# Two-layer stream encoder on one core: keys split once, one reciprocal per head, 9 dummy products, a planner that keeps engines apart at a bank

## The chip, the cores and the metric

The kernel runs on one core of a Trainium2 chip. The metric is the time of one execution on the device in microseconds (us); lower is better. Engines are named as in the profile: PE (matrix products; PEld its weight loads), DVE, ACT and POOL (elementwise work), SP (issues transfers).

## The reference

The program takes 512 tokens of 1024 values through two attention layers, all in float32. Only what bears on the change is quoted.

```python
def diff_dsa_layer(x, ...):               # layer 0
    proj = rms_norm(x, norm_g) @ w_in
    qa, ka, va, qb, kb, vb, qi, ki, wi, gate = split_cols(proj, L0_SIZES)
    o_a = diff_attention(...)             # 4 heads: softmax - lam * softmax
    o_b = dsa_attention(...)              # 8 heads; an indexer picks 128 keys for each query
    return x + (concat(o_a, o_b) * silu(gate)) @ w_o

def dsa_attention(q, k, v, q_idx, k_idx, w_idx, bias_tab, top_k):
    logits = einsum('bqhd,bkd->bqhk', qi_blk, k_idx)         # ki: one key of 64 for 8 heads
    score = einsum('bqh,bqhk->bqk', w_blk, relu(logits))
    _, sel = lax.top_k(score, top_k)
    s = einsum('bqhd,bqkd->bhqk', q_blk, k_sel) * scale      # kb: one key of 64 for 8 heads
    p = softmax(s + bias)

def mla_attention(q_nope, q_rope, k_nope, k_rope, v):        # layer 1, 16 heads
    s = (einsum(q_nope, k_nope) + einsum(q_rope, k_rope)) * scale
    p = softmax(where(chunk_mask, s, -inf))                  # four tiles of 128 queries
    return einsum('bhqk,bkhd->bqhd', p, v)
```

## The kernel before

All values are float32. A product with full precision is made of three fast ones: an operand is split into a high part (`hi_of`, a copy that rounds, on ACT or DVE) and a low part (`lo_of`, a subtraction of the high part, mostly on DVE), and `mm3` adds high*high, high*low and low*high into one bank. A bank is one of 8 accumulators of 128 rows by 512 words in PSUM; PE writes it and ACT and DVE read it. Where a head has only 64 values, `stacks` lays the high part of a query on one half of the 128 rows and its low part on the other half, by four transfers between places in SBUF (`ra<-ra`), so that two products do the work of three (`stacked_scores`). The keys of these products then have to stand in both halves of the rows.

The kernel is first recorded: every call goes into a list (`Schedule.record`) with what it depends on and a price in ns (`cost`). `Schedule.order` then plays the list with these prices on five queues (PE, ACT, DVE, POOL, and the transfers of SP), starts on each free engine the ready operation that was recorded first (with some shifts by `BIAS`), gives out banks and buffers, and picks the engine where there is a choice (`either`, used by `hi_any`, `lo_any`, `vg`). The instructions are written in the order of these starts. On the chip every engine works through its own list in that order; waits on semaphores keep the dependences, and where two engines read one bank, one of them waits for the other. So a change of a price or of one operation can move instructions all through the program.

The stages in the order of time: values and the sum of squares of layer 0 (PE begins with `WARM` dummy products on zeros while the first data arrive); normalised input `H`; the projection of the two keys (`t_proj`, 24 products into one bank), then of the indexer's queries, of four difference heads, of eight sparse heads. The keys `kb` (rows 0 to 63 of the bank) and `ki` (rows 64 to 127) are split in a loop that makes four pairs of `hi_of` and `lo_of` of 64 rows each. The top-k selection runs on DVE (16 rounds of `max` and `match_replace` for three tiles). Gates and the product with `w_o` end layer 0. Layer 1 makes the latent projections, then 16 heads (`head`): for four tiles of queries the scores, `softmax_rows` (DVE adds the mask and takes the minimum; ACT takes the exponential and its sum), a reciprocal on DVE, `scale_rows` on ACT, then ten transposes on PE, and the products with the values. For every fourth head `rope_q` makes four DVE multiplications on 32 rows each, and for every head one DVE addition on 64 rows joins the two halves of the result (`os_`). The sparse heads of layer 0 end with additions on 64 rows by 128 (32 of them).

Of the kernel before, what the change touches and what calls it, by code (L numbers as in the profile page):

```python
# [23 lines left out]
NT = 4  # L24
# [11 lines left out]

TABLE = 2400.0

WARM = 12

SOON = 14000

# [37 lines left out]
class Buf:  # L80


    def __init__(self, arena, words, kind):
        self.arena, self.words, self.kind = arena, words, kind
        self.users, self.used, self.until, self.at, self.turn = 0, 0, 0.0, None, None


class View:
# [47 lines left out]
def _size(ap):  # L136
    n = 1
    for d in ap.shape[1:]:
        n *= d
    return n  # L140
# [47 lines left out]
class Schedule:  # L188
# [65 lines left out]
    def cost(self, key, name, k, wr, rd):  # L254


        n = max(_size(v) for v in wr + rd) if key != "PE" else _size(wr[0])
        psum = any(v.space == PSUM for v in wr + rd)
        if key == "PE":
            if name == "transpose":  # L260
                return 109.0, False
            rows = {F32R: 1, BF16: 1}.get(rd[0].dtype, 4)
            return max(n * rows / 2.4 + {F32R: 13, BF16: 3}.get(rd[0].dtype, 6), 109.0), False
        if name == "dma_start":
            kb = _size(wr[0]) * wr[0].shape[0] * 4 / 1024
            return ISSUE, (kb, RATES[rd[0].space == DRAM, wr[0].space == DRAM, kb >= 256])
        if key == "ACT":
            extra = 93 * (len(rd) - 1) + (93 if "accum_out" in k else 0)
            return _size(wr[0]) * 0.8333 + (52 if rd[0].space == PSUM else 93) + extra, False
        if key == "DVE":  # L270
            if name == "reciprocal":
                return 8.3 * n + 63, False
            fast = name in ("tensor_copy", "tensor_scalar") and not psum
            port = not psum and name not in ("max", "match_replace", "tensor_reduce", "memset")
            if name == "tensor_scalar" and n == 1:
                return 180.0 if len(rd) > 2 else 70.0, port
            return n * (0.521 if fast else 1.0417) + 68 + 60 * sum(_size(v) == 1 for v in rd if n > 1), port
        if key == "POOL":
            if k.get("op") == ALU.pow:
                return 380.0 + 160 * n, True  # L280
            if name == "tensor_copy" or name == "tensor_scalar" and n > 4:
                return 0.84 * n + 190, True
            if name == "tensor_scalar":
                return 340.0 if len(rd) > 2 else 200.0, True
            per = {"memset": 0.85, "tensor_tensor": 2.1}.get(name, 2.0)
            return per * n + (40 if name == "memset" else 198), True

    def order(self):
# [71 lines left out]
                arrive(j, lambda e: 0.0)  # L360
        now, done, tick = 0.0, 0, itertools.count()
        while done < n:
            progress = False
            if back and back[0][0] <= now:
                while back and back[0][0] <= now:
                    b = heapq.heappop(back)[2]
# [5 lines left out]
            for e in engines:  # L372
# [4 lines left out]
                while pool[e] and free[e] <= now:  # L377
# [6 lines left out]
                        continue  # L384
                    op = ops[j]
                    if e in port and op[9][c][5] and not port_free(now, e, entry):
                        later.append(entry)
                        continue
                    new = [b for b in op[8] if b.at is None]
# [21 lines left out]
                    src = "DMA" if op[1] == "dma_start" else e  # L411
                    for b in op[8]:
                        b.used += 1
                        b.until = max(b.until, end + LAT[src]["PE"])
                        if b.used == b.users:
                            heapq.heappush(back, (b.until, next(tick), b))
# [12 lines left out]
            if not progress:  # L429
                nxt = [free[e] for e in engines if pool[e] and free[e] > now]  # L430
                nxt += [wait[e][0][0] for e in engines if wait[e] and wait[e][0][0] > now]
                nxt += [back[0][0]] if back else []
                nxt += [t for t in port.values() if t > now]
                assert nxt, "no place left"
                now = min(nxt)
        self.pick, self.end = pick, max(finish)
# [14 lines left out]
def encoder_kernel(ctx, tc, x, xt0, xt, rel_bias, w_t0, w_va, lam_v, subln, w_o0,  # L451
# [15 lines left out]
    def R(words, kind="r"):  # L467
        return sched.alloc(ra, words, kind)
# [304 lines left out]
    def t_proj(stream, cols):  # L773
        w = both(stream.next(), lambda v: v.rearrange("p (k m) -> p k m", k=8))
        b = bank("d")
        for k in range(8):
            mm3(by_tile(b), both(w, lambda v: v[:, k]), cols.k(k), k == 0, k == 7)
        return b
# [2 lines left out]
    G.memset(cmn, 0.0)  # L781
    G.memset(cmn[0:64, 448:512], -BIG)

    b = t_proj(wt0, H)
    kst = []
    for r0 in (0, 64):
        hh, ll = R(512), R(512)
        src = b[r0:r0 + 64]
        for rows in (slice(0, 64), slice(64, 128)):
            hi_of(hh[rows], src)  # L790
            lo_of(ll[rows], src, hh[rows])
        kst.append((hh, ll))
    kb, ki = kst

    def full(b, scale, kind="r", via=False):

# [9 lines left out]
        lo_scaled(ll, b, hh, scale) if scale != 1.0 else lo_of(ll, b, hh)  # L806
        return hl

    def halves(hl):
        return hl[:, 0:512], hl[:, 512:1024]  # L810

    def stacks(b, scale, via=False):

# [103 lines left out]


    mark_dsa = len(sched.ops)
    osum = [F(512) for _ in range(4)]  # L920
    for i in range(NT):
        n = 128 * (i + 1)
# [236 lines left out]
    def head(h, q, vs):  # L1159
        kk = halves(kbuf[h % NK])  # L1160
        hv = h % 8
        prs = []
        for i in range(NT):
            n = 128 * (i + 1)
            sb = bank("s")
            if i:
                mm3(sb[:, 0:n], both(q, lambda v: v[:, tok(i)]), both(kk, lambda v: v[:, 0:n]), True, True)
            else:

                qf, kf = F(128, "qf"), F(128, "qf")  # L1170
                for f, (hh, ll) in ((qf, q), (kf, kk)):
                    vg(lambda e: e.tensor_tensor(out=f, in0=hh[:, 0:128], in1=ll[:, 0:128], op=ALU.add))
                T.matmul(sb[:, 0:128], qf, kf, start=True, stop=True)
            sd, rc = sm(1), sm(1)
            p = softmax_rows(sb, n, mz[:, 512 - n:512], sd)
            V.reciprocal(rc, sd)
            scale_rows(p, rc)
            prs.append(p)

        def turn(blocks, pair):  # L1180
            bt = bank("t")
            for c, (kt, i) in enumerate(blocks):
                T.transpose(bt[:, tok(c)], prs[i][:, tok(kt)], ident)
            bt = bt[:, 0:128 * len(blocks)]
            hi_any(pair[0], bt)
            lo_of(pair[1], bt, pair[0])

        ob = bank("o")
        zz = pbz[h % 2]
        pa, pc = (R(512, "pa"), R(512, "pa")), (R(256, "pc"), R(256, "pc"))  # L1190
        turn([(0, i) for i in range(4)], pa)
        turn([(3, 3), (1, 1), (1, 2), (1, 3)], both(zz, lambda v: v[:, 128:640]))
        turn([(2, 2), (2, 3)], pc)
        parts = [(0, 0, pa), (1, 128, both(zz, lambda v: v[:, 256:640])), (2, 256, pc),
                 (3, 256, both(zz, lambda v: v[:, 0:256]))]
        for kt, o, pair in parts:
            mm(ob[:, o:512], vs[kt][:, hv], pair[0], kt == 0, False)
            mm(ob[:, o:512], vs[kt][:, hv], pair[1], False, kt == 3)
        return ob
# [173 lines left out]
```

## Time and profile before

| | us |
|---|---|
| median of 3 runs (lowest, highest) | 533.37 (532.03, 534.36) |
| the profiled execution | 533.3 |
| its span, first to last instruction | 531.5 |
| PE busy, DVE busy, ACT busy, POOL busy | 520.9, 436.1, 322.7, 128.8 |

The profiled execution's own time is 1.8 us longer than its span and agrees with the median. Busy time of PE is the union of modelled intervals, in which products overlap; busy times of the other engines are sums of instructions.

### The profile page before, as it was taken

Reading aid. Unit: us, or ns where it says so; the run is one execution under the profiler, and the core shown is the slowest. Engines: PE = TensorE matmul, PEld = TensorE weight load, DVE = VectorE, ACT = ScalarE, POOL = GpSimd, SP = SyncE. Lnnn points to the kernel's source line nnn. Section 1 sums busy time; section 2 is a strip of 40 time slices with the busy share of each in tenths; the row PEclk is TensorE's granted clock in tenths of the full one; section 3 lists DMA queues with packets and bytes.
Section 4 is the critical chain, followed back from the end, with each engine's and each line's share of the span. In section 5 each row is a group of like instructions: output and inputs, shape, how many; then the busy total and the mean of one; then the engine's idle time right before and its main releaser. Section 6 shows DMA issues by size and latency. Waiting matters only on the chain.

```text
span 531.5 us, 8612 instructions
## 1 busy us (share of the span) xinstructions
PE 520.9 (98%) x2770; PEld 440.4 (83%) x2770; DVE 436.1 (82%) x1099; ACT 322.7 (61%) x745; POOL 128.8 (24%) x193
## 2 busy tenths in 40 slices
PE   9999899999999999999999999999999999999995
PEld 6998788888788888787889998888888887888885
DVE  5878779999999999669489457799899888998744
ACT  6655662785787976673244235289868858995011
POOL 1010001431447544210012114322231201410311
PEclk9999999999999999999999999999999999999999
DMA  8463657539446014019366103953753535846012
GB/s 287 168 206 102 175 136 201 129 109 255 111 121 182 7 40 159 1 41 349 129 240 208 41 21 99 213 138 92 179 157 106 146 106 132 230 159 218 2 44 115
DMA packets 30144, 73.80 MB, mean 139 GB/s; under 512 B 4072, under 2 KB 9364, under 8 KB 30100
## 3 DMA queue, kind: packets, MB, share of 16 engines
q1 hardware_dynamic: 29812, 72.73, 46.7%
q8 instruction: 22, 0.36, 0.3%
q10 hardware_dynamic: 288, 0.53, 0.3%
q14 instruction: 22, 0.18, 0.1%
HBM read 45.96 MB, written 4.80 MB: 96 GB/s over the span
## 4 chain that ended last, share of the span: by engine, by line
PE 75%; DVE 15%; ACT 5%; issue 3%; DMA 1%; POOL 0%; POOLq 0%; DVEq 0%; ACTq 0%
PE bank L443 75%; DVE fa L443 8%; DVE ra L443 5%; ACT fa L443 4%; DVE ring L443 2%; ACT ra L443 1%; DMA ra<-ra 1%; POOL fa L443 0%; POOLq L1369 0%; POOL ring L443 0%; DVE warm L443 0%; DVEq L1369 0%; ACT ring L443 0%; DVEq L443 0%; ACTq L443 0%
## 5 line engine op out<-in xcount | busy, mean ns | idle before, releaser
L443 PE MATMUL bank<-ra 128*128 128x512 f32 (+4 forms) x2276 | 493.3, 369 | 2.1 <-DMA ra<-ra 1.7
L443 PEld LDWEIGHTS bank<-ra 128*128 128x128 f32 x2276 | 385.5, 189 | 62.4 <-issue 2.5
L443 ACT ACTIVATE fa<-fa,ring 128x128 f32<-128x128 f32 (+3 forms) x244 | 127.5, 557 | 65.4 <-POOL ring L443 32.5
L443 ACT ACTIVATE ra<-fa 128x1024 fp32r<-128x1024 f32 (+7 forms) x121 | 90.3, 771 | 47.0 <-PE bank L443 21.0
L443 DVE TENSOR_TENSOR ra<-fa,ra 128x512 fp32r<-128x512 f32 (+4 forms) x153 | 103.7, 708 | 12.1 <-ACT ra L443 10.7
L443 ACT ACTIVATE fa<-bank 128x512 f32<-128x512 f32 (+4 forms) x106 | 52.0, 500 | 43.6 <-PE bank L443 41.5
L443 DVE TENSOR_TENSOR ra<-bank,ra 128x512 fp32r<-128x512 f32 (+2 forms) x100 | 59.1, 624 | 11.4 <-ACT ra L443 10.5
L443 ACT ACTIVATE ra<-bank 128x512 fp32r<-128x512 f32 (+3 forms) x84 | 45.6, 561 | 36.4 <-PE bank L443 32.0
L443 DVE TENSOR_TENSOR fa<-bank,fa 64x128 f32<-64x128 f32 (+6 forms) x97 | 46.3, 484 | 23.6 <-PE bank L443 20.1
L443 PE MATMUL bank<-ident,fa 128*128 128x128 f32 x352 | 64.0, 274 | 1.1 <-ACT fa L443 0.7
L443 POOL TENSOR_TENSOR fa<-fa 128x256 f32<-128x256 f32 (+3 forms) x49 | 46.7, 960 | 61.3 <-DVE fa L443 42.5
L443 POOL TENSOR_TENSOR ra<-fa,ra 128x512 fp32r<-128x512 f32 (+1 forms) x26 | 33.5, 1296 | 108.9 <-ACT ra L443 101.0
L443 DVE CUSTOM_DVE_ANT_0 fa<-bank,fa 128x128 f32<-128x128 f32 (+3 forms) x128 | 57.8, 479 | 0.8 <-issue 0.2
L443 PEld LDWEIGHTS bank<-ident,fa 128*128 128x128 f32 x352 | 44.5, 140 | 14.3 <-ACT fa L443 4.9
L443 POOL TENSOR_TENSOR ring<-ring,mhalf 128x1 f32<-128x1 f32 (+1 forms) x20 | 14.5, 724 | 74.6 <-DVE ring L443 73.6
L443 POOL TENSOR_TENSOR fa<-ra 128x128 f32<-128x128 f32 x28 | 14.9, 535 | 65.1 <-DMA ra<-ra 36.9
L443 DVE MATCH_REPLACE8 fa<-ring,fa 128x256 f32<-128x256 f32 (+2 forms) x48 | 25.7, 538 | 0.0
L443 DVE MAX8 ring<-fa 128x8 f32<-128x256 f32 (+2 forms) x48 | 25.2, 547 | 0.2
L443 DVE CAST ra<-bank 128x512 fp32r<-128x512 f32 (+1 forms) x36 | 21.4, 618 | 4.1 <-PE bank L443 3.8
L443 ACT ACTIVATION_READ_ACCUMULATOR fa<-fa,ring 128x1 f32 x128 | 24.3, 190 | 0.0
L443 PEld LDWEIGHTS bank<-fa 128*128 128x128 f32 (+1 forms) x114 | 16.7, 188 | 4.1 <-ACT fa L443 0.9
L443 PE MATMUL bank<-fa 128*128 128x128 f32 (+1 forms) x114 | 19.0, 283 | 0.3 <-ACT fa L443 0.2
(55 smaller groups left out, 195.8 us busy)
## 6 DMA issues: line engine op xcount, KB each, us to landing
ra<-ra SPq DMA_DIRECT2D x64, 256.0 KB, 4.9
fa<-in_w_t_dram SPq DMA_DIRECT2D x25, 512.0 KB, 4.5
fa<-in_w_o_dram SPq DMA_DIRECT2D x16, 512.0 KB, 5.5
ra<-ra SPq DMA_DIRECT2D x48, 128.0 KB, 2.5
fa<-in_w_g_dram SPq DMA_DIRECT2D x8, 512.0 KB, 3.7
fa<-in_w_lat_dram SPq DMA_DIRECT2D x4, 672.0 KB, 5.5
fa<-in_w_uq_dram SPq DMA_DIRECT2D x12, 192.0 KB, 3.4
fa<-in_x_dram SPq DMA_DIRECT2D x4, 512.0 KB, 9.1
```

Source lines behind the costliest of these rows:

```text
L443: fn(*[_real(v) for v in a], **{n: _real(v) for n, v in k.items()})
```

## The change

Five edits. `WARM` goes from 12 to 9. The key bank is split once over all 128 rows (`full`), and `ki` and `kb` reach the other half of the rows by transfers of 64 rows by 1024 words: two for `ki`, and later one that puts `kb` over the place of `ki`. In `head` the four sums of a head stand side by side, one reciprocal of 128x4 is taken after the fourth softmax, and the four scalings follow it. In the planner, an operation of ACT or DVE on a bank is held until the other engine's last one on that bank has ended, and a DVE operation that writes fewer than 128 rows costs 95 ns more.

```diff
-WARM = 12
+WARM = 9
...
+        self.last = {}
...
-            return n * (0.521 if fast else 1.0417) + 68 + 60 * sum(_size(v) == 1 for v in rd if n > 1), port
+            return n * (0.521 if fast else 1.0417) + 68 + 95 * (wr[0].shape[0] < 128) + 60 * sum(_size(v) == 1 for v in rd if n > 1), port
...
-            progress = False
+            progress, held = False, []
...
+                    turns = [t + LAT[o][e] for b in op[8] if e != "PE" for o, t in b.last.items() if o != e]
+                    if turns and max(turns) > now:
+                        held.append(max(turns))
                         later.append(entry)
                         continue
...
+                        if isinstance(b.arena, Banks) and e != "PE":
+                            b.last[e] = end
...
-                nxt += [t for t in port.values() if t > now]
+                nxt += [t for t in port.values() if t > now] + held
...
-    b = t_proj(wt0, H)
-    kst = []
-    for r0 in (0, 64):
-        hh, ll = R(512), R(512)
-        src = b[r0:r0 + 64]
-        for rows in (slice(0, 64), slice(64, 128)):
-            hi_of(hh[rows], src)
-            lo_of(ll[rows], src, hh[rows])
-        kst.append((hh, ll))
-    kb, ki = kst
...
+    kall = full(t_proj(wt0, H), 1.0)
+    kix = R(1024)
+    for o in (0, 64):
+        dma(kix[o:o + 64], kall[64:128])
+    ki = halves(kix)
...
     mark_dsa = len(sched.ops)
+    dma(kall[64:128], kall[0:64])
+    kb = halves(kall)
...
-            sd, rc = sm(1), sm(1)
-            p = softmax_rows(sb, n, mz[:, 512 - n:512], sd)
-            V.reciprocal(rc, sd)
-            scale_rows(p, rc)
-            prs.append(p)
+            if i == 0:
+                sd, rc = sm(4), sm(4)
+            prs.append(softmax_rows(sb, n, mz[:, 512 - n:512], sd[:, i:i + 1]))
+        V.reciprocal(rc, sd)
+        for i in range(NT):
+            scale_rows(prs[i], rc[:, i:i + 1])
```

Over the program the counts change by little else: PE has 2702 products for 2705 (the three dummies), SP has three more transfers of 64x1024, DVE has 16 reciprocals of 128x1 for 80 and 28 of 128x4 for 12. The order changes on every engine from the keys on.

On DVE the low parts of the keys were four operations of 64x512 and are one of 128x512; the low part of the first indexer queries, which stands behind them, has three DVE operations between it and `lamneg` where it had five.

On SP at the split of the keys (`ra<-ra 64x512` are the stacks of the indexer's queries, four for each bank; `64x1024` the keys; `in_w_t` weights), before:

```order
L443 DMA fa<-in_w_t_dram 128x1024 x3
L443 DMA ra<-ra 64x512 x2
L443 DMA fa<-in_w_t_dram 128x1024
L443 DMA ra<-ra 64x512 x6
L443 DMA fa<-in_w_t_dram 128x1024 x2
L443 DMA ra<-ra 64x512 x4
```

and of the change:

```order
L453 DMA fa<-in_w_t_dram 128x1024 x3
L453 DMA ra<-ra 64x1024 x2
L453 DMA fa<-in_w_t_dram 128x1024
L453 DMA ra<-ra 64x512 x4
L453 DMA ra<-ra 64x1024
L453 DMA ra<-ra 64x512 x4
L453 DMA fa<-in_w_t_dram 128x1024
```

Two key transfers now go ahead of the first stacks, and the move of `kb` stands between the first and the second four.

On PE from the projections of the first queries (`bank_75`, `bank_73`, `bank_70`) to the first scores of the indexer (`128x256`, `128x384` and `128x512` x2 are the scores of one head), before:

```order
L443 MATMUL bank_75<-ra 128x512 x8
L443 MATMUL bank_73<-ra 128x512 x24
L443 MATMUL bank_70<-ra 128x512 x11
L443 MATMUL bank_76<-ra 128x256 x2
L443 MATMUL bank_77<-ra 128x384 x2
L443 MATMUL bank_74<-ra 128x512 x2
```

and of the change:

```order
L453 MATMUL bank_75<-ra 128x512 x8
L453 MATMUL bank_73<-ra 128x512 x24
L453 MATMUL bank_70<-ra 128x512 x17
L453 MATMUL bank_76<-ra 128x256 x2
L453 MATMUL bank_77<-ra 128x384 x2
L453 MATMUL bank_74<-ra 128x512 x2
```

Six more products of the third projection stand ahead of the first scores.

On DVE in the first heads of layer 1 (`ISA fa,ring` is the mask and minimum of one tile of a softmax, its width the last number; `32x512` are multiplications of `rope_q`), before:

```order
L443 ISA fa,ring<-bank_73,fa 128x512
L443 ISA ring 128x1
L443 RECIPROCAL ring<-ring 128x1
L443 ISA fa,ring<-bank_70,fa 128x256
L443 ISA ring 128x1
L443 ISA fa,ring<-bank_74,fa 128x128
L443 ISA ring 128x1
L443 RECIPROCAL ring<-ring 128x1
L443 TENSOR_TENSOR fa<-bank_72,fa 32x512 x2
L443 RECIPROCAL ring<-ring 128x1
L443 ISA fa,ring<-bank_73,fa 128x384
```

and of the change:

```order
L453 TENSOR_TENSOR fa<-bank_77,fa 32x512
L453 ISA fa,ring<-bank_71,fa 128x128
L453 ISA ring 128x1
L453 ISA fa,ring<-bank_76,fa 128x512
L453 ISA ring 128x1
L453 ISA fa,ring<-bank_72,fa 128x256
L453 ISA ring 128x1
L453 ISA fa,ring<-bank_74,fa 128x128
L453 ISA ring 128x1
L453 TENSOR_TENSOR ra<-bank_73,ra 128x512
L453 RECIPROCAL ring<-ring 128x4
```

The reciprocals that stood one by one behind their tiles became one, which stands behind the first two tiles of the next head. On PE the first transpose of a head stands 53 products behind the head's first score on average over the 16 heads, where it stood 37 behind.

## Rows read from the trace of the kernel before

**Rows 1.** The page, busy time: us, share of the span, instructions.

```profile
PE 520.9 (98%) x2770; PEld 440.4 (83%) x2770; DVE 436.1 (82%) x1099; ACT 322.7 (61%) x745; POOL 128.8 (24%) x193
```

**Rows 2.** Busy time by stretch: us, PE, PEld, DVE, ACT, POOL, granted clock, DMA.

```profile
62.00:220.00 158.00, 157.21 (x824) 131.10 (x822) 148.05 (x430) 109.81 (x291) 58.07 (x94) 1.00 0.45 124
340.00:490.00 150.00, 149.08 (x807) 124.38 (x806) 136.88 (x376) 116.98 (x283) 35.31 (x43) 1.00 0.56 153
500.00:510.00 10.00, 10.00 (x46) 8.28 (x45) 2.50 (x7) 0.00 (x0) 1.17 (x1) 1.00 0.00 0
```

**Rows 3.** Waits of PE and PEld, 50 to 62 us: total us, times, longest.

```profile
PEld bank L443 <- issue: 2.1, 1, 2.1
PE bank L443 <- DMA ra<-ra: 1.7, 1, 1.7
```

**Rows 4.** Waits of PEld, 62 to 220 us.

```profile
PEld bank L443 <- ACT fa L443: 2.6, 5, 0.7
PEld bank L443 <- DVE fa L443: 1.2, 3, 0.4
```

**Rows 5.** Waits of PEld, 340 to 490 us.

```profile
PEld bank L443 <- ACT fa L443: 3.2, 12, 0.6
PEld bank L443 <- DVE ra L443: 1.9, 6, 0.5
PEld bank L443 <- issue: 1.2, 3, 0.5
```

**Rows 6.** The dummies (tile warm): ns min/median/max, first and last start.

```profile
L443 PE MATMUL bank<-warm x12: 606/634/635, 1.2 to 5.8; 128*128 128x512 bf16 x12
```

**Rows 7.** Busy time by stretch at the start (columns as in rows 2).

```profile
5.90:6.90 1.00, 1.00 (x5) 0.91 (x4) 0.92 (x2) 0.47 (x1) 0.00 (x0) 1.00 1.05 364
7.00:8.00 1.00, 1.00 (x10) 1.00 (x10) 0.17 (x1) 0.20 (x1) 0.00 (x0) 1.00 0.92 261
```

**Rows 8.** Timeline of ACT and DVE, 3.5 to 9.4 us: start, length, instruction, idle before.

```profile
3.88 1.03 ACT L443 ACTIVATE ra<-fa 128x256 fp32r<-128x256 f32 x2 [1.43 <-DMA fa<-in_w_va_dram]
7.80 0.72 ACT L443 ACTIVATE ra<-fa 128x512 fp32r<-128x512 f32 x1 [1.43 <-DMA fa<-in_xt_dram]
...
4.94 0.75 DVE L443 SCALAR_TENSOR_TENSOR ra<-fa,ra 128x512 fp32r<-128x512 f32 x1 [0.19 <-ACT ra L443]
```

**Rows 9.** Timeline of ACT, DVE, SP and PE, 44 to 57 us.

```profile
44.37 1.18 ACT L443 ACTIVATE ra<-bank 64x512 fp32r<-64x512 f32 x2
46.30 0.59 ACT L443 ACTIVATE ra<-bank 64x512 fp32r<-64x512 f32 x1 [0.75 <-DVE ra L443]
...
50.42 0.69 DVE L443 TENSOR_TENSOR ra<-bank,ra 128x512 fp32r<-128x512 f32 x1
51.03 1.28 DVE L443 TENSOR_TENSOR ra<-fa,ra 128x512 fp32r<-128x512 f32 x2
...
51.14 3.72 SPq L443 DMA_DIRECT2D ra<-ra  x6
...
55.79 4.43 PE L443 MATMUL bank<-ra 128*128 128x256 f32 x23 [1.73 <-DMA ra<-ra]
```

**Rows 10.** The chain that ended last, 30 to 57 us: start, length, what.

```profile
51.14 4.51 DMA ra<-ra
```

**Rows 11.** Groups of instructions by form: busy us, mean ns, idle before.

```profile
L443 DVE TENSOR_TENSOR fa<-bank,fa 64x128 f32<-64x128 f32 x32 | 9.0, 282 | 0.8 <-ACT fa L443 0.4
L443 DVE RECIPROCAL ring<-ring 128x1 f32<-128x1 f32 x80 | 10.7, 152 | 1.9 <-ACT fa L443 1.1
L443 ACT ACTIVATE fa<-fa,ring 128x384 f32<-128x384 f32 x60 | 35.7, 606 | 6.1 <-DVE ring L443 6.0
```

**Rows 12.** Timeline of DVE, 433 to 445 us.

```profile
435.24 3.48 DVE L443 TENSOR_TENSOR fa<-bank,fa 128x512 f32<-128x512 f32 x5
...
443.97 0.16 DVE L443 RECIPROCAL ring<-ring 128x1 f32<-128x1 f32 x1
444.05 0.68 DVE L443 CUSTOM_DVE_ANT_0 fa<-bank,fa 128x512 f32<-128x512 f32 x1
```

More of the change, by code (lines that the diff above doesn't have):

```diff
@@ L386, in order @@
                     if e in port and op[9][c][5] and not port_free(now, e, entry):
+                        later.append(entry)
+                        continue
+                    turns = [t + LAT[o][e] for b in op[8] if e != "PE" for o, t in b.last.items() if o != e]
+                    if turns and max(turns) > now:
+                        held.append(max(turns))
                         later.append(entry)
@@ L782, in encoder_kernel, with halves @@
     G.memset(cmn[0:64, 448:512], -BIG)
-    b = t_proj(wt0, H)
-    kst = []
-    for r0 in (0, 64):
-        hh, ll = R(512), R(512)
-        src = b[r0:r0 + 64]
-        for rows in (slice(0, 64), slice(64, 128)):
-            hi_of(hh[rows], src)
-            lo_of(ll[rows], src, hh[rows])
-        kst.append((hh, ll))
-    kb, ki = kst
+    def halves(hl):
+        return hl[:, 0:512], hl[:, 512:1024]
     def full(b, scale, kind="r", via=False):
@@ L807, in full @@
         return hl
-    def halves(hl):
-        return hl[:, 0:512], hl[:, 512:1024]
+    kall = full(t_proj(wt0, H), 1.0)
[3 more added lines that the diff above has]
+    ki = halves(kix)
     def stacks(b, scale, via=False):
```

## The prediction

> **What bounds the kernel now.** I read the busy times of the page first: PE is busy in 98% of the span, the next engine, DVE, in 82% [rows 1]. A busy PE is not yet a PE at its peak, so I then looked for a stretch in which nothing is waited for. From 500 to 510 us PE runs products of 512 columns alone, 46 in 10 us, one per 0.217 us [rows 2], which is 512 columns at the 2.4 GHz level of its clock, granted 1.00. So the question is how far the other stretches fall short, and the waits of PE and of its weight loads tell it: one wait of 1.7 us at the first indexer scores [rows 3], some small ones in the attention of layer 0 [rows 4], 3.8 us in the two rows shown, and some in layer 1 [rows 5], 6.3 us in three rows. That is about 12 us of 531.5. Everything else is PE's own work, of which the change removes three dummies and nothing more.
>
> There is a rule that would read this otherwise. The Trainium skill, Perfetto Trace Analysis, section "Identifying the Most-Contended Engine", says that matmul busy time is a bad measure of headroom and that the busy share of the weight loads should be taken. By that rule the 83% of the weight loads would leave 17%, an estimate of 90 us to gain, against some 12 us by the waits. The trace sides with the waits: in the stretch that runs at one product per 0.217 us the weight loads are busy 8.28 of 10 us, so 83% is what a full PE shows here.
>
> In layer 1 DVE is busy 136.9 of 150 us and ACT 117.0, in the attention of layer 0 DVE 148.1 of 158 [rows 2]: the waits of PE there are waits for engines that run late against a list that expected them earlier.
>
> **The change part by part.** The sum is made against the profiled execution's own 533.3 us (span 531.5 and 1.8 around it), practically the median of 533.37.
>
> *Three dummies fewer.* Twelve dummies start between 1.2 and 5.8 us [rows 6], one per (5.8 - 1.2) / 11 = 0.42 us, half the speed of the stretch at 500 us, so on the 1.2 GHz level. The first real products are as slow: 5 start from 5.90 to 6.90, 10 from 7.00 to 8.00 [rows 7]. The granted clock is given as 1.00 in both rows, but the rate doubles, so the level rose to 2.4 GHz near 6.95 us, after 5.8 us of unbroken work. With nine dummies PE is free at 1.2 + 9 x 0.42 = 5.0 us. The first products need high parts only, and those are there at 3.88 + 1.03 = 4.91 [rows 8]; the low part of the activations is there at 4.94 + 0.75 = 5.69, behind six products that do without it (6 x 0.21 = 1.3 us, so no stall). Real work starts 1.2 us earlier. If the clock still rises at 6.95, these 1.2 us run at half speed and give 0.6 us. The next chunk's activations are not there before 7.80 + 0.72 = 8.52 [rows 8], about when PE would now turn to them, so I let that take back a third. I take **-0.4 us**. Bounds: -1.3 (three dummies at 0.42) if real work ran at full speed at once; +0.6 if the clock rose 2 us later, each such us costing half a us.
> Here a rule of the Trainium skill bears on the sign: TensorE: Matmul & The Clock Gate, section "Part 1: The HAM clock gate", says that the moment of the rise is set by a window that runs freely and not by how many products went before, and that it differs from run to run. By it the rise stays where it is and this edit is worth -0.6 to -0.4; if the rise instead needed the same work as before, by the rows, it would be worth about nothing. No run so far shows which.
>
> *The keys split once.* Before, ACT and DVE take turns at the key bank: four pairs from 44.37 on, and ACT idles 0.75 us for DVE at each handover [rows 9]. The low part of the first queries comes only at 50.42, its transfers are issued at 51.14 and land 4.51 us later [rows 10], and PE starts the first scores at 55.79, after 1.73 us of waiting [rows 9]. Of the four pairs one stays: one high part of about 0.6 us on ACT and one low part of 0.6 to 0.7 on DVE. With the high part from about 44.4 to 45.1 the key's low part runs to about 46.2, two low parts of weights to 47.4 (0.6 apart, from the pair of 1.28 us [rows 9]), and that of the queries to 48.1, 3 us earlier than before (50.42 + 0.69). Its transfers, behind two key transfers, land at about 48.7 + 4.5 = 53.2. The keys themselves, issued by 46.8, land by 51.3 at the same 4.5 us. PE asks for both only after six more products, 6 x 0.22 = 1.3 us after the place where it stalled, near 55.3. So the stall goes: **-1.9 us** (1.73 of idle time and the restart of the weight loads; they wait 2.1 [rows 3]). Bounds: -1.9 and 0, if the transfers landed 2 us later than I think. A gain beyond it is excluded, since PE has its own work from there on. The later move of `kb` makes SP wait until the keys have landed (about 51.3), with the second pair's four stacks queued behind it: at 0.6 us each (six took 3.72 [rows 9]) they are issued by 53.7 and land by 58.2. PE asks for them after 12 more scores and 12 products, about 2.1 + 12 x 0.22 = 4.7 us after 55.3, at 60.0. It costs nothing, with 1.8 us of cover; without the cover it would cost what it is late.
>
> *One reciprocal per head.* DVE drops 64 reciprocals of 128x1 and gains 16 of 128x4. A reciprocal takes 0.152 us [rows 11] but holds the next instruction up by only 0.08 (443.97 to 444.05 [rows 12]), so 48 fewer free 48 x 0.08 = 3.8 us of DVE in layer 1. In return the scalings of a head come in one burst: three that used to run early now stand before the last one's work, at about 0.5 us each (0.606 for 384 columns [rows 11], less for 256 and 128), 1.5 us later per head. What covers it: PE has on average 53 products between a head's first score and its first transpose, where it had 37; 16 more at some 0.2 us are 3 us.
>
> *New prices and turns in the planner.* An operation on 32 rows is 0.70 us behind the one before it ((3.48 - 0.69) / 4), one on 128 rows 0.59 (1.28 - 0.69, [rows 9]), while the old price was 0.60 for both [rows 12]. So the old list was 0.1 us late at each such place: 16 multiplications of `rope_q` and 16 additions in layer 1, 3 us, and 32 additions of 64x128 in layer 0 (0.282 us each [rows 11]), another 3 us. The new list knows this, and in layer 1 DVE also has 3.8 us less to do. The lateness known by now is of the size of the waits in rows 4 and 5. But waits come back elsewhere in a list that is drawn anew, and more than half of them end with ACT (2.6 and 3.2 us), whose prices stay. I take a fifth of the 3.8 us in layer 0, **-0.7 us**, and a fifth of the 6.3 us in layer 1, **-1.3 us**. These two are choices, not counts. Bounds: all but a third of the waits gone (-2.5 and -4.2), or half as much again (+1.9 and +3.2).
>
> Sum: -0.4 - 1.9 - 0.7 - 1.3 = -4.3, **529.0 us**.
>
> **The rivals.**
> 1. Only the counted parts work (-0.4 and -1.9) and the small waits merely move to other places: 533.3 - 2.3 = 531.0. For it: the planner lays transposes right where it expects their data in either list. Against it: known lateness of 3 us in each layer is now priced in.
> 2. The waits of both attention stages halve: -2.3 - 1.9 - 3.2 = -7.4, 525.9. For it: lateness and waits are of one size. Against it: half of the wait in layer 1 is for ACT.
> 3. The burst of scalings is not covered, and PE waits at the first transpose of each head. Its price is up to 1.5 us x 16 = 24 us; it overturns the gain and makes the kernel slower by over 0.5% where more than (2.3 + 2.7) / 16 = 0.3 us per head are left open. With half a us open: 531.0 + 8 = 539. Against it: 3 us of other work on average. For it: ACT is busy 78% of the stretch, so a burst can meet a queue.
> 4. The clock rises 2 us later, since the dummies end earlier and PE waits some 0.1 us for its first data: +0.6 for -0.4, and the choices at nothing: 533.3 + 0.6 - 1.9 = 532.0. This is the case against which the Trainium skill's rule on the free window (named above) stands.
>
> **How the numbers follow.** Half a per cent, 2.7 us, is about what a measurement of this kernel tells from no change (its three runs spread over 2.3). Chances: forecast 0.48 (its own range 527.3 to 530.6), rival 1 0.28, rival 2 0.11, rival 3 0.06, rival 4 0.07. The range runs from 526.4, inside rival 2's share, to 532.8, past rival 4; it leaves out rival 3 and half of rival 2. Faster than 530.7: all of rival 2, nine tenths of the forecast, a third of rival 1, 0.64. Within the bound: the rest of the forecast, of rival 1 and rival 4, 0.30. Slower: rival 3, 0.06.
>
> **What would show it.** Dummies: nine products at 0.42 us, the first real one near 5.1 us, the doubling of the rate still near 7 us. Keys: no wait of PE for `ra<-ra` near 55 us, ACT without the 0.75 us handovers, the stacks' transfers landed before PE asks. Layer 1: DVE busy about 4 to 7 us less, the weight loads' waits for ACT and DVE under the 6.3 us. Wrong would make it: a new wait of over 1 us at the second stacks near 60 us; waits for ACT at the first transposes of layer 1 that add up to more than before; slow products past 8 us.

## The result and the profile after

| | before | changed |
|---|---|---|
| median (lowest, highest) of nine runs, us | 532.72 (531.66, 534.36) | 528.77 (528.55, 532.19) |
| ratio, 95% interval | | 0.9935 [0.9916, 0.9954] |

The change gains 4.0 us by the medians, 0.74% (0.65% by the means of the nine, which the ratio compares); predicted were 4.3 us below the profiled 533.3, so 529.0. The profiled execution of the changed kernel took 532.19 us (span 530.4), the slowest of its nine; the other eight took 528.55 to 529.92. It shows the mechanisms well, and one of them at its worst. A second profile of the same kernel (e9 below, 529.62 us) stands beside it where that matters.

The page of the changed kernel, busy time, to set against [rows 1]:

```profile
PE 517.7 (98%) x2767; PEld 441.4 (83%) x2767; DVE 429.4 (81%) x1048; ACT 319.0 (60%) x743; POOL 127.4 (24%) x192
```

DVE has lost 6.7 us of work, PE 3.2; PE has the three products fewer. (In the views by stretch the number behind an x counts every instruction that overlaps the stretch, at its edges too.) Busy time by stretch of the changed kernel, to set against [rows 2, 7]:

```profile
62.00:220.00 158.00, 153.41 (x807) 128.17 (x806) 143.02 (x424) 109.50 (x292) 59.37 (x95) 1.00 0.44 119
340.00:490.00 150.00, 149.15 (x815) 126.29 (x814) 136.20 (x329) 116.15 (x285) 34.97 (x43) 1.00 0.57 155
7.00:8.00 1.00, 1.00 (x9) 1.00 (x9) 1.00 (x3) 1.00 (x3) 0.00 (x0) 1.00 0.89 327
```

Two things are to be seen. In layer 1 (340 to 490 us) PE works on 815 products where it worked on 807. In the attention of layer 0 (62 to 220) it works on 807 where it worked on 824, and is busy 3.8 us less: there the change has lost time, which the total hides.

The waits of the weight loads of the changed kernel, 62 to 220 us, to set against [rows 4]:

```profile
PEld bank L453 <- ACT ra L453: 2.8, 2, 1.5
PEld bank L453 <- ACT fa L453: 2.6, 5, 0.8
PEld bank L453 <- POOL fa L453: 1.4, 1, 1.4
PEld bank L453 <- issue: 1.0, 1, 1.0
PEld bank L453 <- DVE ra L453: 0.8, 4, 0.3
PEld bank L453 <- DVE ring L453: 0.2, 1, 0.2
```

and those of 340 to 490 us, to set against [rows 5]:

```profile
PEld bank L453 <- DVE ra L453: 2.9, 8, 1.0
PEld bank L453 <- ACT fa L453: 1.1, 5, 0.3
```

The first list has grown to 8.8 us, where before all its rows made 4.9. The second has shrunk from 6.8 to 4.0, and twelve waits for ACT have become five. At the first indexer scores nothing is left of [rows 3]. In the timeline of PE and the engines that split, 43 to 58 us, the changed kernel, PE runs from 42.72 on through the place of the stall:

```profile
42.72 15.66 PE L453 MATMUL bank<-ra 128*128 128x512 f32 x71
...
43.60 0.60 ACT L453 ACTIVATE ra<-bank 128x512 fp32r<-128x512 f32 x1
...
46.88 0.68 DVE L453 TENSOR_TENSOR ra<-bank,ra 128x512 fp32r<-128x512 f32 x1
47.03 6.89 SPq L453 DMA_DIRECT2D ra<-ra  x9
```

One pair of splits of the keys (its high part at 43.60 on ACT) stands where four stood [rows 9], the queries' low part is done at 46.88 + 0.68 = 47.56 where it was done at 51.11, and their transfers go out from 47.03. That is the predicted course, half a us earlier than forecast (48.1). What followed was not forecast. The timeline of the changed kernel, 58 to 80 us:

```profile
59.05 2.88 SPq L453 DMA_DIRECT2D ra<-ra  x4
...
61.97 8.35 SPq L453 DMA_DIRECT2D fa<-in_w_t_dram  x2
...
64.48 10.58 PEld L453 LDWEIGHTS bank<-ra 128*128 128x128 f32 x50 [1.00 <-issue]
64.52 10.97 PE L453 MATMUL bank<-ra 128*128 128x256 f32 x50 [0.61 <-DMA ra<-ra]
...
66.70 3.26 DVE L453 SCALAR_TENSOR_TENSOR fa<-fa,wn 128x256 f32<-128x256 f32 x6
...
70.43 8.76 SPq L453 DMA_DIRECT2D ra<-ra  x8
...
75.07 1.06 ACT L453 ACTIVATE ra<-fa 128x1024 fp32r<-128x1024 f32 x1 [5.11 <-DMA fa<-in_w_t_dram]
...
76.40 3.78 PEld L453 LDWEIGHTS bank<-ra 128*128 128x128 f32 x20 [1.34 <-ACT ra L453]
76.44 3.94 PE L453 MATMUL bank<-ra 128*128 128x256 f32 x19 [0.95 <-DMA ra<-ra]
```

PE waits at 64.5 for stacks that left from 59.05 on, and again at 76.4. There ACT has stood idle for 5.11 us until a fetch of weights (`in_w_t`) landed; SP had issued it near 61.97 + 8.35 - 0.3 = 70.0, and the stacks that PE waits for at 76.4 left SP behind it, from 70.43 on. SP had stood still before it. Its own waits, 60 to 72 us, the changed kernel:

```profile
SPq L453 <- DVE fa L453: 6.9, 2, 6.3
```

The longest of them, 6.3 us, ends at this fetch. By the profile it was released by DVE at work in the buffers `fa`, into which the weights go; the group of DVE above ends at 66.70 + 3.26 = 69.96. So the fetch stood at the head of SP's queue until a buffer came free. The waits of 62 to 110 us, the changed kernel, sum it up:

```profile
ACT ra L453 <- DMA fa<-in_w_t_dram: 11.3, 3, 5.1
...
PE bank L453 <- DMA ra<-ra: 2.6, 3, 1.1
```

### The profile page after: what moved, and what is told of

The parts are those of the page before. It is cut to its first block, busy times and chain, and to the rows that moved or that the text cites. A ratio compares the mean times of both kernels' runs of the same rounds, so it can differ in the third digit from the quotient of the medians.

```text
span 530.4 us, 8562 instructions
## 1 busy us (share of the span) xinstructions
PE 517.7 (98%) x2767; PEld 441.4 (83%) x2767; DVE 429.4 (81%) x1048; ACT 319.0 (60%) x743; POOL 127.4 (24%) x192
## 5 line engine op out<-in xcount | busy, mean ns | idle before, releaser
L453 DVE TENSOR_TENSOR ra<-fa,ra 128x512 fp32r<-128x512 f32 (+4 forms) x153 | 101.3, 690 | 18.3 <-ACT ra L453 16.6
L453 ACT ACTIVATE ra<-fa 128x512 fp32r<-128x512 f32 (+7 forms) x116 | 85.8, 762 | 47.5 <-PE bank L453 16.0
L453 ACT ACTIVATE ra<-bank 128x512 fp32r<-128x512 f32 (+2 forms) x87 | 46.5, 558 | 44.0 <-PE bank L453 41.3
L453 DVE TENSOR_TENSOR ra<-bank,ra 128x512 fp32r<-128x512 f32 (+2 forms) x97 | 57.5, 623 | 12.4 <-ACT ra L453 12.0
L453 PE MATMUL bank<-ident,fa 128*128 128x128 f32 x352 | 60.3, 273 | 0.9 <-POOL fa L453 0.9
L453 DVE CUSTOM_DVE_ANT_0 fa<-bank,fa 128x512 f32<-128x512 f32 (+3 forms) x128 | 58.0, 482 | 2.9 <-PE bank L453 2.3
L453 POOL TENSOR_TENSOR fa<-fa 128x256 f32<-128x256 f32 (+3 forms) x47 | 42.8, 915 | 60.1 <-DVE fa L453 38.0
L453 DVE CAST ra<-bank 128x512 fp32r<-128x512 f32 (+1 forms) x30 | 18.0, 621 | 8.8 <-PE bank L453 8.7
```

Of the source, the lines that this page charges most:

```text
L453: fn(*[_real(v) for v in a], **{n: _real(v) for n, v in k.items()})
```

## The experiments

All are compared with the kernel before on the same chip; its medians there were 532.35 (e1 to e4), 532.20 (e5 to e8) and 532.38 (e9 to e12). First each part alone.

**e1, the dummies alone.** The lists of before are kept to the instruction, and three dummies are not issued:

```diff
+ISSUED = 9
...
+            if j in self.skip:
+                continue
...
+        if j >= ISSUED:
+            sched.skip.add(len(sched.ops))
```

> The lists of before are kept on every engine; only three of the twelve dummies are not issued. Theory (the clock rises at its own moment): first real product near 5.1 us, the rate of PE doubles near 6.95 us as before, time 532.7 - 0.4 = 532.3 us, between -0.7 and -0.2. Rival (the rise needs the same work as before): the doubling comes 1 us or more later and the time stays within 0.2 us of before or rises.

Measured: 531.72 (530.98 to 532.32), ratio 0.9988 [0.9979, 0.9997], 0.6 us less. Predicted were 0.4. The rate of PE doubled neither near 6.95 us, as expected, nor later, as the rival has it, but earlier. The stretch from 5 to 6 us (PE, granted clock, DMA) of the kernel before, then of this run:

```profile
5.00:6.00 1.00, 1.00 (x5) 1.00 1.04 372
5.00:6.00 1.00, 1.00 (x8) 1.00 1.03 374
```

**e2, the keys alone.** One split, two transfers for `ki`, one for `kb`; the prices and turns of before.

```diff
-            hi_of(hh[rows], src)
-            lo_of(ll[rows], src, hh[rows])
...
+    kall = full(t_proj(wt0, H), 1.0)
...
+        dma(kix[o:o + 64], kall[64:128])
...
+    dma(kall[64:128], kall[0:64])
```

> Before with the keys split once and moved by transfers, nothing else. Theory: the wait of PE for the first stacks near 54 us (1.7 us) is gone and the time falls by 1.9 us to 530.8. Rival (a redrawn list deals its waits anew, or transfers queued behind the key moves come late): the wait near 54 us is gone, but others of 1 us or more stand at the second or third stacks (60 to 95 us), and the time falls by less than 0.7 us.

Measured: 532.41 (531.12 to 533.77), ratio 1.0005 [0.9995, 1.0014]: nothing, where 1.9 us were predicted. The stall at 55 us is gone, and other waits have come. Those of the weight loads of this run, 62 to 220 us:

```profile
PEld bank L443 <- ACT fa L443: 3.9, 8, 0.9
PEld bank L443 <- POOL fa L443: 1.3, 1, 1.3
...
```

With the smaller rows they make 7.9 us, 3.0 more than before.

**e3, the reciprocal alone**, with the order that it brings (one of 128x4, then four scalings).

```diff
-            V.reciprocal(rc, sd)
-            scale_rows(p, rc)
...
+        V.reciprocal(rc, sd)
+        for i in range(NT):
+            scale_rows(prs[i], rc[:, i:i + 1])
```

> Before with one reciprocal of 128x4 for a head of layer 1, nothing else. Theory: DVE 4 to 7 us less busy, waits of the weight loads between 340 and 490 us under 6.3 us, time down by about 0.8 us (half of the 1.3 us taken for layer 1). Rival (the burst of scalings is not covered): waits for ACT at first transposes grow past 3.2 us and the time rises by 1 us or more.

Measured: 530.16 (529.50 to 530.74), ratio 0.9961 [0.9948, 0.9973], 2.2 us less. The weight loads' waits in layer 1 (340 to 490 us) of this run are 2.6 us shorter than before, and the burst of scalings has brought no new one:

```profile
PEld bank L443 <- ACT fa L443: 2.7, 10, 0.5
PEld bank L443 <- DVE ra L443: 1.3, 4, 0.4
PEld bank L443 <- ACT ra L443: 0.2, 1, 0.2
```

**e4, the planner alone**: turns at a bank and the price of narrow operations.

```diff
-            return n * (0.521 if fast else 1.0417) + 68 + 60 * sum(_size(v) == 1 for v in rd if n > 1), port
+            return n * (0.521 if fast else 1.0417) + 68 + 95 * (wr[0].shape[0] < 128) + 60 * sum(_size(v) == 1 for v in rd if n > 1), port
...
+                    if turns and max(turns) > now:
+                        held.append(max(turns))
...
```

> Before with the planner's two edits (turns at a bank, 95 ns more for under 128 rows), the computation as it was. Theory (lateness now priced in): waits of the weight loads in 62 to 220 and 340 to 490 us fall, time down by about 1.2 us. Rival (waits only move): the time stays within 0.7 us of before.

Measured: 528.49 (527.86 to 528.80), ratio 0.9929 [0.9916, 0.9941]: 3.9 us less, as much as the whole change.

Now the change with a part taken out.

**e5, all but the keys**: the changed kernel with the old loop over four pairs.

```diff
-    kall = full(t_proj(wt0, H), 1.0)
...
+            hi_of(hh[rows], src)
+            lo_of(ll[rows], src, hh[rows])
```

> The change without its edit on the keys (they are split in four pairs as before); dummies, reciprocal and both planner edits stay. Theory (once the planner knows that engines take turns at a bank, it lays the four pairs so that no stall is left at the first scores, and the edit on the keys only brings new waits of PE for ra<-ra between 60 and 110 us): those waits are gone, 526.5 us, between 525.5 and 527.5, so 2 us under the whole change. Rival (the edit on the keys gives its 1.9 us in this list as well): 530.5 us, above the whole change.

Measured: 527.69 (527.07 to 528.12), ratio 0.9913 [0.9898, 0.9929], 4.5 us less: the best version of all, though not the 526.5 expected. The four pairs are still there, but the planner that knows the turns no longer lets the engines alternate. Timeline of this run, 43 to 58 us:

```profile
42.73 15.50 PE L453 MATMUL bank<-ra 128*128 128x512 f32 x73
...
43.61 3.03 ACT L453 ACTIVATE ra<-bank 64x512 fp32r<-64x512 f32 x5
...
46.05 3.52 DVE L453 TENSOR_TENSOR ra<-bank,ra 64x512 fp32r<-64x512 f32 x5 [0.33 <-ACT ra L453]
46.66 7.21 SPq L453 DMA_DIRECT2D ra<-ra  x8
```

The high parts run in a row on ACT, the low parts in a row on DVE, the stacks go out from 46.66 on, and PE does not stall. SP's own queue in this run, 40 to 80 us, in which the fetches leave at 55.4, 55.9, 63.9 and 69.1, where the changed kernel's left at 57.2, 62.0, 70.0 and 79.2:

```profile
...
55.42 0.81 SPq L453 DMA_DIRECT2D fa<-in_w_t_dram  x2
61.17 2.66 SPq L453 DMA_DIRECT2D ra<-ra  x4
63.94 0.52 SPq L453 DMA_DIRECT2D fa<-in_w_t_dram  x1
66.61 2.40 SPq L453 DMA_DIRECT2D ra<-ra  x4
69.05 0.58 SPq L453 DMA_DIRECT2D fa<-in_w_t_dram  x1
...
```

Here no fetch waits long for a buffer. SP's own waits for DVE on `fa` in this run, 60 to 72 us, are

```profile
SPq L453 <- DVE fa L453: 0.5, 1, 0.5
```

Its busy time by stretch:

```profile
62.00:220.00 158.00, 157.83 (x830) 132.17 (x829) 148.35 (x430) 108.41 (x290) 57.90 (x93) 1.00 0.44 117
340.00:490.00 150.00, 148.96 (x812) 126.07 (x811) 136.70 (x332) 116.32 (x283) 28.96 (x36) 1.00 0.56 151
```

830 products in the attention of layer 0, against 807 in the changed kernel; in layer 1 the two are close (812 and 815).

**e6, all but the planner.** The changed kernel without what e4's diff adds.

> The change without both planner edits; dummies, keys and reciprocal stay. Theory (the planner carries the change): no lower than 529.5 us, about 530.4, with the waits at 75 to 108 us as with the keys alone. Rival (the parts are worth the same in any list, and the planner alone took 3.9 us of 532.35): dummies and reciprocal, 0.6 and 2.2 us, hold in full and keys give nothing, 529.5 us.

Measured: 530.33 (529.55 to 533.56), ratio 0.9976 [0.9959, 0.9993], 1.9 us less by the medians and 1.3 by the means. Eight of its twelve runs lie between 529.5 and 531.1 and four above 532.

**e7, the turns alone**, the planner's half without the price.

```diff
...
+                    if turns and max(turns) > now:
+                        held.append(max(turns))
...
```

> Before with only the rule that an engine is held until the other one has left the bank; the price of operations on under 128 rows stays as it was. Theory: the four highs of the keys stand together on ACT and the four lows on DVE, the wait near 54 us is gone, time down by about 2 us, to 530.4; the waits in layer 1 stay at 5 us or more, since its 32-row operations are still priced too low. Rival (the price of 95 ns carries the planner's gain): within 0.7 us of before.

Measured: 531.63 (530.87 to 532.14), ratio 0.9988 [0.9977, 0.9998], 0.6 us less where 1.8 were expected. The stall at 55 us is gone in this run too, but the waits of layer 1 rise by 1.3 us (table below).

**e8, the whole change with a higher price of an issue.** On SP the six transfers of [rows 9] start (3.72 - 0.5) / 5 = 0.64 us apart, taking about 0.5 for the last; the planner reckons 0.48.

```diff
-ISSUE, FIRST, LAST, LANES = 480.0, 1400.0, 550.0, 8
+ISSUE, FIRST, LAST, LANES = 620.0, 1400.0, 550.0, 8
```

> The whole change with the planner's price of issuing one transfer raised from 480 to 620 ns; in the trace of the change the transfers ra<-ra follow each other at a median of 0.64 us. Theory (the waits of PE for ra<-ra at 63, 75 and 92 us come from transfers priced too low, so that scores stand too early in the list): these three waits fall from 3.1 us together to under 1, time 526.5 us. Rival (the waits come with any list that has the moved keys): they stay or move, 528 to 530 us.

Measured: 529.66 (529.47 to 529.97), ratio 0.9952 [0.9937, 0.9967]. PE's waits for `ra<-ra` fall under 1 us, as expected, but the time gains nothing. In 62 to 110 us ACT's waits for fetched weights fall from the changed kernel's 11.3 us to 3.4, and PE's for stacks from 2.6 to 0.4, here of this run:

```profile
ACT ra L453 <- DMA fa<-in_w_t_dram: 3.4, 2, 2.5
...
PE bank L453 <- DMA ra<-ra: 0.4, 1, 0.4
```

The fetch that left at 70.0 leaves at 64.9 here, and SP's waits for DVE on `fa`, 60 to 72 us, have shrunk:

```profile
SPq L453 <- DVE fa L453: 1.3, 2, 0.9
```

But in layer 1, drawn anew, the weight loads wait 5.4 us instead of 4.0.

**e9, the change once more**, unaltered, to see what of its first profile is the kernel and what the run.

> The whole change once more, for a profile of an execution near its median (the one taken with the result lasted 532.19 us, the median was 528.77). Theory (the 3.4 us between them are waits of PE for late transfers and weights between 60 and 110 us): time 528.8 us, and in the profile the waits of the weight loads and of PE for ra<-ra, ACT ra and POOL between 62 and 110 us are 3 us or more lower than in that profile, the rest alike. Rival (these waits stand in every execution): they are the same and the difference is spread over the span.

Measured: 529.54 (527.86 to 532.20), ratio 0.9953 [0.9931, 0.9974]; the profiled run took 529.62. The weight loads' waits of this run from 62 to 220 us make 6.8 us in all, less than the 8.8 of the first profile and more than the 4.9 of before. So the loss in this stretch belongs to the kernel, and its size varies from run to run. Of the 2.6 us between the two profiles these waits are 2.0; the rest is elsewhere, part of it in the first ten microseconds (last section).

**e10, the price alone**: only the term `95 * (wr[0].shape[0] < 128)`.

> Before with the price alone (95 ns more on DVE for under 128 rows). Theory (turns alone took 0.6 us of the planner's 3.9, the price brings the rest, in layer 1 above all, where 32 operations of 32 and 64 rows were late): 529.2 us, waits of the weight loads in 340 to 490 us under 5 us. Rival (each of the two alone gives little and only the list drawn with both happens to be good): 531.5 us or more.

Measured: 529.42 (529.17 to 530.21), ratio 0.9946 [0.9934, 0.9959], 3.0 us less. The waits of layer 1 fall to 5.4 us, not under 5 as expected (table below). Most of what the planner gives comes with one number in its table of prices.

**e11, the burst with four reciprocals.** The order of e3, but four of 128x1, so that DVE saves nothing.

```diff
-        V.reciprocal(rc, sd)
+        for i in range(NT):
+            V.reciprocal(rc[:, i:i + 1], sd[:, i:i + 1])
```

> Before with the order of the reciprocal edit, but four reciprocals of 128x1 behind the fourth softmax in the place of one of 128x4: the burst of scalings without the saved time on DVE. The edit itself took 2.2 us. Theory (the gain is DVE's saved 3.8 us): within 0.7 us of before, 532 us. Rival (the gain is that reciprocals no longer stand between the tiles, or the list drawn anew): 530.2 us, as with the one reciprocal.

Measured: 531.49 (530.81 to 532.30), ratio 0.9983 [0.9974, 0.9992], 0.9 us less, between the two expectations. So of e3's 2.2 us 0.9 come with the other order or the redrawn list, which this run does not part, and some 1.3 with the single reciprocal: with DVE's saved time, or with the list drawn for it, which is not e11's.

**e12, all but the reciprocal**: the changed kernel without e3's lines.

> The change without its edit on the reciprocal. Theory (planner and reciprocal take the same waits of layer 1, so they overlap; dummies and planner alone sum to 4.5 us, keys cost about 1): 529.0 us, within 0.8 us of the whole change. Rival (the reciprocal keeps its 2.2 us in any list): 530.9 us.

Measured: 528.56 (527.84 to 529.41), ratio 0.9928 [0.9914, 0.9941], 3.8 us less. Taking the reciprocal out of the change costs nothing that can be measured, though alone it gives 2.2.

**All of them side by side.** The weight loads' waits, in us, each number the sum of all rows of that view in the stretch, in the profiled run of the kernel; the time of that run; and the median:

| kernel | 50 to 62 | 62 to 220 | 220 to 340 | 340 to 490 | sum | profiled run | median |
|---|---|---|---|---|---|---|---|
| before | 2.1 | 4.9 | 0.8 | 6.8 | 14.6 | 533.3 | 532.72 |
| e1 dummies | 1.4 | 4.6 | 0.7 | 6.8 | 13.5 | 531.23 | 531.72 |
| e2 keys | 0 | 7.9 | 0.6 | 6.5 | 15.0 | 533.77 | 532.41 |
| e3 reciprocal | 1.4 | 5.1 | 0.5 | 4.2 | 11.2 | 530.05 | 530.16 |
| e11 burst of four | 1.6 | 4.9 | 0.5 | 5.6 | 12.6 | 532.30 | 531.49 |
| e7 turns | 0 | 4.6 | 0.6 | 8.1 | 13.3 | 531.58 | 531.63 |
| e10 price | 1.2 | 3.9 | 0.8 | 5.4 | 11.3 | 529.82 | 529.42 |
| e4 planner | 0 | 3.4 | 0 | 5.7 | 9.1 | 528.80 | 528.49 |
| e6 all but planner | 0 | 8.4 | 0.6 | 4.5 | 13.5 | 532.20 | 530.33 |
| e12 all but reciprocal | 0 | 4.3 | 0 | 5.4 | 9.7 | 528.62 | 528.56 |
| e8 change, issue 620 | 0 | 4.1 | 0 | 5.4 | 9.5 | 529.69 | 529.66 |
| e9 change again | 0 | 6.8 | 0 | 3.9 | 10.7 | 529.62 | 529.54 |
| changed | 0 | 8.8 | 0 | 4.0 | 12.8 | 532.19 | 528.77 |
| e5 all but keys | 0 | 3.6 | 0 | 4.0 | 7.6 | 527.75 | 527.69 |

The sum follows the time of the profiled run: no row leaves the line through before (14.6 us and 533.3) and e5 (7.6 and 527.75) by more than 1.2 us. The first 50 us, left out here, hold 4.4 to 5.1 us of such waits in every kernel. So in this kernel the time is won and lost in small waits of PE, and a stretch can be read by itself, to about that 1.2 us. Every kernel with the moved keys that has a twin with the old loop has more in the second column than the twin (e2 against before, e12 against e4, which still has twelve dummies, changed and e9 against e5), by 0.9 to 5.2 us. In e2, e6, e12, e9 and the changed kernel one wait of SP for DVE on `fa` between 60 and 72 us lasts 5.7 to 6.3 us; in e8 none is over 0.9, in the kernels with the old loop of which this was read (before, e1, e4, e5, e7) none over 0.5.

## Why the prediction was right, and where it was not

The total was right: 4.0 us measured in nine runs (2.8 in e9) for 4.3 predicted. The reading that stood behind it was right too: PE is full where nothing is waited for, only waits can be gained, and the whole span of results lies within the 12 us of waits counted. (The 46 products of [rows 2] take in those that overlap an edge. From start to start they are 0.227 us apart, not 0.217, as their line in the timeline of PE gives it, (10.59 - 0.39) / 45, with 0.39 for the last:

```profile
499.62 10.59 PE L443 MATMUL bank<-ra 128*128 128x512 f32 x46
```

For 512 columns 2.4 GHz would be 0.213 us; what takes the rest no run here shows. The argument stays.) But the terms were not right, and made up for one another; that they add up so near to the measured total is luck. e9's row of the table, against that of before, gives what became of each: the stall -2.1 (-1.9 predicted), layer 0's attention +1.9 (-0.7), the stretch from 220 to 340 us -0.8 (no term), layer 1 -2.9 (-1.3); with the dummies' -0.6 (-0.4) that makes -4.5, where the two profiled runs lie 3.7 apart.

**Dummies, -0.4.** Right in sign and nearly in size: -0.6 in e1, with an interval of 0.2 to 1.1. The nine dummies start from 1.2 to 4.6 us, the changed kernel's first real product at 4.89 (5.1 was forecast):

```profile
L453 PE MATMUL bank<-warm x9: 607/634/634, 1.2 to 4.6; 128*128 128x512 bf16 x9
```

Rival 4 (a rise of the clock 2 us later) did not come: from 7.00 to 8.00 us 9 products overlap the stretch, where 10 did [rows 7]. But the sum took the rise to stay at 6.95 us. In this run it came near there, in e1 and e9 before 6 us (last section), so the size is in part luck.

**Keys split once, -1.9.** This is the step that failed. Its mechanism was right (the stall goes, and by the route described), but it was booked to an edit that is worth nothing: alone it measured 0 (e2), and in the whole change it costs 1.1 us (e5 at 527.69 against 528.77) to 1.8 (against e9's 529.54); the intervals of e5 and of the change overlap a little, those of e5 and e9 do not. The step "it costs nothing, with 1.8 us of cover" failed. It followed only the move of `kb` and the stacks straight behind it, and named "a new wait of over 1 us at the second stacks near 60 us" as what would make it wrong. A wait came, 4 us later, at stacks behind these (at 64.5 us, 0.6 of PE and 1.0 of its weight loads), and more waits after it, where weights arrived late because their fetches had been issued 2 to 10 us later than in e5, the one of 70.0 after 6.3 us at the head of SP's queue. The stall itself also goes by the turn rule alone (e4, e7, e5), which the prediction did not see: it had taken the alternation of ACT and DVE for a matter of four pairs, where it was one of the order in which a planner without turns laid them. And the stall was no fixed 1.9: runs with the same list there show 1.4 and 1.6 us (e1, e3, e11).

**Layer 0's attention, -0.7.** Too small where the keys stay (4.9 to 3.4 us of waits in e4, 3.6 in e5), and of the wrong sign in the changed kernel (6.8 and 8.8), for the reason above.

**Layer 1, -1.3.** Right in sign and mis-sized: the weight loads' waits fall from 6.8 us to 4.0, by 2.8. The chosen fifth of 6.3 us was nearer two fifths. That DVE is 6.7 us less busy (4 to 7 forecast) shows little: the figure is of the whole program, in 340 to 490 us it falls by 0.7 [rows 2], and e5, with the same reciprocals and the best time, has DVE busy for 438.9 us, 2.8 more than before, since the planner also picks anew which engine does what. The reciprocals themselves did shrink, over the program from 12.7 us to 7.1. The reason given for the new price holds in part only. Of the 16 additions on 64 rows those that write rows 0 to 63 hold the next operation no longer than one on 128 rows does (last section), so half of the lateness counted for these additions was not there; what e10 shows is that the new price gives a better list. The waits for ACT went as well, from 3.2 to 1.1, though no price of ACT changed; the prediction had counted them against a larger gain. Both the price (6.8 to 5.4 in e10) and the reciprocal (to 4.2 in e3) empty this column, and the second of them finds less left: 5.4 to 4.0, and nothing in the median (e12). That fits the sum of the parts, -0.6, 0, -2.2 and -3.9, which is -6.7 where the whole gives -4.0: the key edit takes one or two, and without it e5 gives 4.5 of the 6.7, since the reciprocal and the planner share the same waits.

**The rivals.** Rival 1 (the small waits merely move) falls with e10 and e3: each takes waits away that do not come back. Rival 2 (both stages halve, 525.9) holds for neither stage in full; e5 at 527.69 is what there is of it. Rival 3 (the burst is not covered, 539) falls with e3 and e11: the burst is in both, and both are faster.

**What stays open.** The traces show why the fetches go later in the lists with the moved keys: one of them stands at the head of SP's queue for some 6 us, for a buffer that DVE still works in, and what is queued behind it waits too. A higher price of an issue removes this wait and most of the loss in that stretch (8.8 or 6.8 us to 4.1 in e8, against 3.6 in e5), so the planner's price of SP's queue is part of why it laid the fetch there; whether more buffers would do the same no run here shows. And how much of a gain is a better price and how much a lucky drawing of the list, single lists cannot tell: e11's 0.9 us is such a case.

## What to carry to other kernels

Where a planner writes the order, an edit has two prices, its own work and the new list, so time it alone and also leave it out of the whole; here the second test found a version 1.1 us better than the change (e5). A wrong price in the planner is an edit worth looking for first: 95 ns on narrow operations gave more than any change of the work here (3.0 us against 2.2 at most). When a transfer moves forward in an in-order queue, follow every later transfer of that queue, not just the next one: what buffer it waits for, and who uses what stands behind it.

## What the runs showed of the hardware

**The rise of TensorE's clock came at different moments in two runs of one kernel.** Products of the changed kernel between 5.2 and 6.8 us, by form (busy us, mean ns of one, idle before):

```profile
L453 PE MATMUL bank<-ra 128*128 128x256 f32 x8 | 2.1, 436 | 0.0
```

and those of the same kernel in e9, whose first real product was 0.2 us later (5.11 for 4.89):

```profile
L453 PE MATMUL bank<-ra 128*128 128x256 f32 x10 | 1.9, 302 | 0.0
```

The first works there on the 1.2 GHz level, the second mostly on that of 2.4, with nine dummies behind both. In the trace of the first the products of 256 columns last 415 ns and start 0.21 us apart up to 6.55 us; in e9 they last 282 and start 0.12 apart from 5.44 on. The granted clock is given as 1.00 in all this time, as in [rows 7]. The Trainium skill, TensorE: Matmul & The Clock Gate, section "Part 1: The HAM clock gate", says that the window which sets the moment of the rise runs freely against the program and that the moment varies between runs. The traces agree: here at least 6.55 - 5.44 = 1.1 us lie between the two moments.

**On DVE it is not the number of rows that keeps operations apart.** In e5 four operations of 64x512 and one of 128x512 behind them took 3.52 us, (3.52 - 0.69) / 4 = 0.71 apart; 128 rows take 0.59 [rows 9]. The 95 ns of the new price come near this difference. But the additions on 64 rows of layer 1 write, in the order of the heads, rows 0 to 63 for one head and rows 64 to 127 for the next, and the operations behind them come at two distances, in the same turn. Timeline of DVE, the kernel before, one addition of either kind and the operation behind it (from 426.9 to 428 and from 431.9 to 433.2 us):

```profile
426.94 0.68 DVE L443 TENSOR_TENSOR fa<-bank,fa 64x512 f32<-64x512 f32 x1 [0.54 <-ACT fa L443]
427.55 0.67 DVE L443 CAST ra<-bank 128x512 fp32r<-128x512 f32 x1
...
431.91 0.69 DVE L443 TENSOR_TENSOR fa<-bank,fa 64x512 f32<-64x512 f32 x1
432.63 0.43 DVE L443 TENSOR_TENSOR ra<-fa,ra 128x256 fp32r<-128x256 f32 x1
```

They are 0.61 us and 0.72. So it is in the whole trace: behind the first kind 0.60 to 0.61 us where DVE did not stand idle (six of eight), behind the second 0.71 to 0.72 (eight of eight), which is 0.03 longer than the operation itself. So the number of rows alone does not make the distance; which rows they are does. That it is where they start against the operation beside it fits these rows, and is not shown further.

**Late fetches and spread.** The changed kernel's runs lie 3.6 us apart and e9's 4.3, those of e5 1.1 and of e8 0.5. In the first two ACT waits about 11 us for fetches between 62 and 110 us, in e8 3.4 and in e5 not at all; e6 (11.2 us, 4.0 apart) goes with the first two, e2 (10.0 us) lies 2.7 apart. That a landing which varies makes the spread is argued from this, not shown; the kernel before waits 0.4 for them and lies 2.7 apart all the same.
